# A two-layer encoder trunk on one core: the gates' way through HBM, all transposes of x in the norm's stretch, and two row blocks ordered by token half

## The chip, the cores and the metric

The kernel runs on one core of one Trainium2 chip. The metric is the device time of one execution in microseconds; the time shown is the median of several runs. TensorE (PE) multiplies; its weight loads are listed as PEld. VectorE (DVE) and ScalarE (ACT) do the element-wise work, SyncE (SP) and GpSimd (POOL) issue DMA transfers.

## The reference

256 tokens, model width 2048, two layers, all in float32. A conditioning vector gives six vectors per layer (shift, scale and gate for attention and for the MLP). Cut to what matters here:

```
cond = silu(c)
for l in range(2):
    sh_a, sc_a, g_a, sh_m, sc_m, g_m = split(cond @ w_ada[l] + b_ada[l], 6)
    h = rmsnorm(x) * (1 + sc_a) + sh_a
    proj = h @ w_in[l]                      # q, k, v of 4 differential heads; latents of 8 MLA heads
    out_a = diff_attention(...)             # two softmax maps per head, relative bias
    out_b = mla_attention(...)              # latent q and kv, rope
    x = x + g_a * (concat(out_a, out_b) @ w_o[l])
    h = rmsnorm(x) * (1 + sc_m) + sh_m
    x = x + g_m * (square(relu(h @ w_mlp_in[l])) @ w_mlp_out[l])
return rmsnorm(x) * final_norm_g
```

## The kernel before

**Precision.** Most products run as three matmuls on a faster 4-byte format: a weight block is split into a rounded high part (`hi`, made by ACT, line 151) and the rest (`lo`, made by DVE, line 154), and so is the activation; then hi·hi, hi·lo and lo·hi are added up. A weight block is 1 MB in a `raw` buffer (five of them, shared with the ada rows), and its parts live in four `hi` and four `lo` buffers of half a block each.

**Modulation.** The six vectors per layer come from `w_ada`: 192 rows of 1 MB, each loaded by SP (line 357), multiplied by the conditioning vector and summed on DVE (line 373), then added to the bias into `mod` (lines 385 and 387), 128 features per column. Loads are rationed: each call of `weights` adds a rate (`RATE_*`, by stage) to a credit in `more_ada`, and each whole credit loads one row; the sums are made at the next call.

**Row products.** The attention output projection (`w_o`) and the MLP's second product (`w_m2`) are made by `rows`: for each of four column groups `c` of 512, four weight blocks `kq`, and for both token halves `t` of 128 tokens (one PSUM bank each), eight high and four low matmuls of 512 columns per block and half (lines 309, 310, 312). Then `updates` multiplies by the gate row and adds to x on DVE (lines 1107, 1109), and ahead of a norm ACT squares the new x and sums it (line 1123). For the last column group (`last`), `first_squares` and `quiet` (no ada) apply, and in the last block all matmuls of half 0 come ahead of those of half 1. In this layout x has tokens on the partitions; `self.row` holds the gate on all 128 partitions, in the buffer that otherwise holds the relative bias.

**Gates.** `gate` brings `mod` (128 x 16) into HBM, element by element in transposed order, and reads it back over all partitions. Both transfers are POOL's. There are four of them: g_a and g_m of two layers.

**The norm between.** `norm_then_by_k` runs three times: ahead of the first MLP, of the second layer's attention and of the second MLP. x is turned back to features on partitions by PE transposes (line 1156; `turned(p)` makes four, for features 256 p to 256 p + 255, into one PSUM bank, and copies the bank to SBUF by ACT or DVE, lines 1165 and 1163). The root of each token half (`roots`: ACT square root, line 1137, DVE reciprocal, line 1140) is spread over the partitions by a matmul (`spread_one`, line 1144). `modulated` then makes h for 256 features: DVE scales (line 695), ACT adds the shift and rounds (line 698), DVE makes the rest (line 701). Eight such steps follow, each with its weight blocks: in layer 0 two blocks, by `by_k`; in layer 1 one, by `wide_by_k`, in which the low weights of all six banks come first in the very first step. Transposes 0 to 3 stand ahead of the second spread, 4 and 5 behind it and ahead of the first step's products, 6 and 7 one each ahead of the products of steps 1 and 2. PSUM has eight banks in rotation.

**Order.** The framework lists the instructions of each engine by its own cost model and the program's order, with transfers of SP among them: what is ready early can be issued ahead of its place in the program. `behind(a, b)` pins `a` behind `b` on an engine's list without a wait. Each engine then works its list in order.

**Start.** In the first layer x is loaded and turned ahead of the projection; for the residual it is loaded a second time with tokens on the partitions (line 976), and the relative bias is kept in HBM for layer 1 (line 974), by POOL.

**End.** `final` follows the last `rows`: last norm and eight output transfers of 128 x 512 values, four per token half.

Of the kernel before, what the change touches and what calls it, by code (L numbers as in the profile page):

```python
# [9 lines left out]
F32 = mybir.dt.float32  # L10
# [87 lines left out]
RATE_A0, RATE_V, RATE_A1, RATE_A2, RATE_K, RATE_K1, RATE_M = 1.1, 1.6, 0.5, 0.7, 0.6, 0.0, 0.66  # L98
# [3 lines left out]
class Trunk:  # L102
# [26 lines left out]
    def s(self, name, n=2):  # L129
        return self.sp.tile([P, n], F32, tag=f"s{n}", name=self.name(name))  # L130
# [60 lines left out]
    def mac(self, ps, w, c, m, x, first, last, shared=False):  # L191
        mm = self.nc.tensor.matmul
        hi, lo = w[0][:, c : c + m], w[1][:, c : c + m]
        mm(ps, hi, x[0], start=first, stop=False, skip_group_check=shared)  # L194
        mm(ps, hi, x[1], start=False, stop=False, skip_group_check=shared)  # L195
        self.last_mac = mm(ps, lo, x[0], start=False, stop=last, skip_group_check=shared)  # L196
# [48 lines left out]
    def by_k(self, banks, blocks, xs, k0, nk, n=4, whole=None):  # L245


        for b, (w, half) in enumerate(blocks):
            for i in range(len(w) * half // (n * P)):
                k = k0 + i  # L250
                for j in range(n):
# [7 lines left out]
                    else:  # L259
                        self.mac(ps, w[c // half], c % half, P, xs[k], first, last, True)  # L260
                if i == 0 and not whole:
                    self.last_mm = self.last_mac

    def wide_by_k(self, banks, blocks, xs, k0, nk):

        mm = self.nc.tensor.matmul
        n = len(banks)
        (w, half), = blocks
        for i in range(2 * half // (n * P)):
            k = k0 + i  # L270
            x, _, both = xs[k]
            part = lambda j, h: w[(i * n + j) * P // half][h][:, (i * n + j) * P % half :][:, :P]
            for h in (1, 0) if k == 0 else (0, 1):
                for j, ps in enumerate(banks):
                    if h:
                        mm(ps[:, 0], part(j, 1), x, start=k == 0, stop=k == nk - 1, skip_group_check=True)
                    else:
                        ins = mm(  # L278
                            ps.rearrange("p a b -> p (a b)"), part(j, 0), both, start=False, stop=False,
                            skip_group_check=True,  # L280
                        )
            if i == 0:
                self.last_mm = ins
# [12 lines left out]
    def rows_by_k(self, pss, src, xs, kq, apart=False):  # L296

        mm = self.nc.tensor.matmul
        w = self.weights(src)
        part = lambda i, h: w[i // 2][h][:, i % 2 * 512 : i % 2 * 512 + 512]  # L300
        for ts in ((0,), (1,)) if apart else ((0, 1),):
            for h in range(2):
                for i in range(4):
                    for t in ts:
                        ps = pss[t].rearrange("p a b -> p (a b)")
                        c = slice(t * P, (t + 1) * P)
                        xh, xl, _ = xs[4 * kq + i]
                        if h == 0:
                            mm(ps, xh[:, c], part(i, 0), start=kq == 0 and i == 0, stop=False)  # L309
                            mm(ps, xl[:, c], part(i, 0), start=False, stop=False)  # L310
                        else:
                            self.last_mm = mm(ps, xh[:, c], part(i, 1), start=False, stop=kq == 3 and i == 3)  # L312
# [375 lines left out]
    def modulated(self, x, r, k, sh, sc, after=None):  # L688
# [4 lines left out]
        for i, (hi, lo, _) in enumerate(out):  # L693
# [166 lines left out]
    def layer(self, l, acc=None):  # L860
# [112 lines left out]
        if l == 0:  # L973
            nc.gpsimd.dma_start(self.bias_kept, self.row)
            for t in range(2):
                nc.gpsimd.dma_start(self.xr[:, t], io["x"][t])
# [23 lines left out]
        self.rows_by_k(pss, io["w_o"][l, 0, 0], self.mo, 0)  # L1000
        for f in (av[0][1], av[1][1], av[2][0], av[3][0]):
            f()
        self.rows_by_k(pss, io["w_o"][l, 0, 1], self.mo, 1)
# [409 lines left out]
```

## Time and profile before

| | |
|---|---|
| median of 3 runs | 2195.16 us (2195.14 to 2196.54) |
| the profiled execution | 2194.0 us, its span 2191.8 us |
| PE busy | 2148.8 us, 98% of the span |
| DVE, ACT busy | 1590.6 us, 73%; 1141.8 us, 52% |
| HBM read, written | 589.66 MB, 3.18 MB |
| mean granted TensorE clock | 0.995 |

Matmuls run back to back nearly everywhere. The span holds, in order: the first norm and projection (to about 140 us), the rest of attention 0 with its output projection (to 413.5), norm and first MLP (to 1126.7), norm and attention 1 (to 1471.2), norm and second MLP (to 2182.4), last norm and output. A row of a group reads: line, engine, operation, output<-input, count, busy time; a bracket behind an instruction of the timeline holds the idle time of its engine before it and what ended it.

### The profile page before, as it was taken

How to read it: one execution, taken by the hardware profiler on the slowest of the kernel's cores; microseconds unless marked ns; L12 is line 12 of the kernel's file. 1: busy time of each engine (PE TensorE's matmuls, PEld its weight loads, DVE VectorE, ACT ScalarE, POOL GpSimd, SP SyncE). 2: the span in 40 equal slices, each digit the busy share in tenths (PEclk: the TensorE clock that was granted, in tenths of full speed). 3: DMA queues.
4: the chain of work that ended last, by engine and by line, in shares of the span. 5: the costliest groups of instructions: out<-in, count | busy, mean ns of one | idle time of the engine just before them, and what ended most of it. 6: DMA issues, size and time to landing. Idle time of an engine off the chain costs nothing.

```text
span 2191.8 us, 29356 instructions
## 1 busy us (share of the span) xinstructions
PE 2148.8 (98%) x11498; PEld 1861.3 (85%) x11498; DVE 1590.6 (73%) x2114; ACT 1141.8 (52%) x1724; POOL 11.1 (1%) x22
## 2 busy tenths in 40 slices
PE   7999999999999999999999999999999999999998
PEld 6899778898888888888889998888888888888886
DVE  7789778888778978887976776778655555555555
ACT  6555554555455355445454565547535534644643
POOL 0000000000000000000000000000000000000000
PEclk9999999999999999999999999999999999999999
DMA  9997898799988888889967766767864555555552
GB/s 386 423 386 290 258 354 323 287 342 344 289 329 333 326 304 322 328 305 295 346 231 259 260 234 228 261 222 251 296 235 175 202 196 179 192 200 184 192 196 93
DMA packets 87307, 594.76 MB, mean 271 GB/s; under 512 B 9984, under 2 KB 10368, under 8 KB 20352
## 3 DMA queue, kind: packets, MB, share of 16 engines
q1 hardware_dynamic: 85536, 583.93, 73.7%
q0 software_dynamic: 1344, 8.42, 1.0%
q8 instruction: 90, 1.47, 0.3%
q10 hardware_dynamic: 288, 0.52, 0.1%
q14 instruction: 49, 0.40, 0.0%
HBM read 589.66 MB, written 3.18 MB: 270 GB/s over the span
## 4 chain that ended last, share of the span: by engine, by line
PE 89%; DMA 5%; DVE 4%; ACT 1%; issue 1%; SPq 0%; ACTq 0%; DVEq 0%
PE ps L215 18%; PE pr L309 13%; PE pr L310 13%; PE pr L312 13%; PE ps L218 9%; PE pk L258 2%; PE pk L278 2%; PE pk L194 2%; PE pk L195 2%; PE pk L196 2%; DMA raw<-in_w_m 2%; DVE ada L373 1%; PE pv L293 1%; PE pv L294 1%; PE pv L292 1%; DMA w<-in_w_d 1%
## 5 line engine op out<-in xcount | busy, mean ns | idle before, releaser
L154 DVE TENSOR_TENSOR lo<-raw,hi 128x1024 fp32r<-128x1024 f32 (+1 forms) x714 | 836.0, 1195 | 434.4 <-issue 218.9
L151 ACT ACTIVATE hi<-raw 128x1024 fp32r<-128x1024 f32 (+1 forms) x714 | 733.4, 1036 | 724.2 <-PE pr L310 376.0
L373 DVE SCALAR_TENSOR_TENSOR ada<-ada,cond 128x2048 f32<-128x2048 f32 x192 | 438.7, 2287 | 17.9 <-DMA ada<-in_w_ada 17.5
L215 PE MATMUL ps<-h,hi 128*128 128x512 f32 x1856 | 432.1, 390 | 0.8 <-ACT hi L151 0.8
L215 PEld LDWEIGHTS ps<-h,hi 128*128 128x128 f32 x1856 | 344.9, 188 | 71.1 <-ACT hi L151 1.7
L310 PE MATMUL pr<-hi,hid 128*128 128x512 f32 x1024 | 398.5, 389 | 0.0
L309 PE MATMUL pr<-hi,hid 128*128 128x512 f32 x1024 | 398.4, 389 | 0.0
L312 PE MATMUL pr<-lo,hid 128*128 128x512 f32 x1024 | 253.2, 389 | 0.0
L218 PEld LDWEIGHTS ps<-h,lo 128*128 128x128 f32 x1856 | 230.3, 192 | 4.5
L218 PE MATMUL ps<-h,lo 128*128 128x256 f32 x1856 | 231.7, 283 | 0.0
L312 PEld LDWEIGHTS pr<-lo,hid 128*128 128x128 f32 x1024 | 192.2, 188 | 39.9
L310 PEld LDWEIGHTS pr<-hi,hid 128*128 128x128 f32 x1024 | 192.2, 188 | 39.7
L309 PEld LDWEIGHTS pr<-hi,hid 128*128 128x128 f32 x1024 | 192.2, 188 | 39.7
L194 PE MATMUL pk<-h,hi 128*128 128x256 f32 x320 | 90.3, 285 | 0.2 <-ACT h L698 0.2
L195 PE MATMUL pk<-h,hi 128*128 128x256 f32 x320 | 90.3, 283 | 0.0
L196 PE MATMUL pk<-h,lo 128*128 128x256 f32 x320 | 90.3, 283 | 0.0
L188 DVE TENSOR_TENSOR hid<-relu,hid 128x256 fp32r<-128x256 f32 x128 | 48.3, 422 | 57.0 <-ACT hid L187 57.0
L258 PE MATMUL pk<-hf,w 128*128 128x256 f32 x384 | 84.2, 380 | 3.6 <-DMA w<-in_w_d 3.6
L1175 ACT ACTIVATE sum<-ps 128x256 f32<-128x256 f32 x110 | 40.9, 379 | 89.1 <-PE ps L218 89.0
L258 PEld LDWEIGHTS pk<-hf,w 128*128 128x128 f32 x384 | 72.5, 190 | 14.2 <-issue 2.6
L1107 DVE TENSOR_TENSOR yg<-pr,bias 128x512 f32<-128x512 f32 x64 | 42.5, 685 | 30.0 <-PE pr L312 29.0
L194 PEld LDWEIGHTS pk<-h,hi 128*128 128x128 f32 x320 | 61.0, 192 | 0.6 <-ACT h L698 0.5
(236 smaller groups left out, 2495.5 us busy)
## 6 DMA issues: line engine op xcount, KB each, us to landing
raw<-in_w_m SPq DMA_DIRECT2D x238, 1024.0 KB, 5.6
ada<-in_w_ada SPq DMA_DIRECT2D x192, 1024.0 KB, 6.4
raw<-in_w_o SPq DMA_DIRECT2D x32, 1024.0 KB, 5.7
raw<-in_w_m SPq DMA_DIRECT2D x24, 768.0 KB, 5.7
raw<-in_w_dv SPq DMA_DIRECT2D x16, 1024.0 KB, 5.8
raw<-in_w_t SPq DMA_DIRECT2D x12, 1024.0 KB, 5.1
w<-in_w_a SPq DMA_DIRECT2D x24, 384.0 KB, 13.6
raw<-in_w_a SPq DMA_DIRECT2D x12, 768.0 KB, 4.9
```

The lines of the kernel that those rows point to most:

```text
L151: ins = self.nc.scalar.activation(hi, v, AF.Copy)
L154: ins = self.nc.vector.tensor_tensor(lo, v, hi.bitcast(F32), ALU.subtract)
L194: mm(ps, hi, x[0], start=first, stop=False, skip_group_check=shared)
L195: mm(ps, hi, x[1], start=False, stop=False, skip_group_check=shared)
L196: self.last_mac = mm(ps, lo, x[0], start=False, stop=last, skip_group_check=shared)
L215: mm(ps.rearrange("p a b -> p (a b)"), part(w, k, 0), x[2], start=k == 0, stop=False)
L218: mm(ps[:, 0], part(w, k, 1), x[0], start=False, stop=k == nk - 1)
L258: self.nc.tensor.matmul(ps, v, whole[k], start=first, stop=last, skip_group_check=True)
L309: mm(ps, xh[:, c], part(i, 0), start=kq == 0 and i == 0, stop=False)
L310: mm(ps, xl[:, c], part(i, 0), start=False, stop=False)
L312: self.last_mm = mm(ps, xh[:, c], part(i, 1), start=False, stop=kq == 3 and i == 3)
L373: ins = nc.vector.scalar_tensor_tensor(w, w, 1.0, self.cond, ALU.mult, ALU.mult, accum_out=acc[:, i : i + 1])
```

## The change

- `gate`: PE transposes `mod` into a PSUM bank, ACT copies the bank to SBUF, and POOL writes that to HBM as 16 rows of 512 bytes. The broadcast back is as before.
- `turned` is parted into `turn_in` (transposes) and `turn_out` (copy). In `norm_then_by_k` all eight sets of transposes stand ahead of the first step: 0, the first spread, 1 to 5, the second spread, 6, 7. ACT copies 5, 6 and 7 after the first step's h. DVE copies 1 and 3, ACT the others. Both parts of the first weight block are split without being held behind the last update of x (before: one, held). The call of `more_ada` in the first step goes.
- `by_k` in the first step (layer 0) starts the second block's tiles behind the last product of the first; `wide_by_k` (layer 1) does the first step in two groups of three banks.
- `rows`, for the last column group: blocks 2 and 3 are both split first; then half 0 with blocks 2 and 3, then half 1 with blocks 2 and 3.
- The bias kept and the second load of x are issued by SP in place of POOL.
- `RATE_M` is 0.7 in place of 0.66.

```diff
-RATE_A0, RATE_V, RATE_A1, RATE_A2, RATE_K, RATE_K1, RATE_M = 1.1, 1.6, 0.5, 0.7, 0.6, 0.0, 0.66
+RATE_A0, RATE_V, RATE_A1, RATE_A2, RATE_K, RATE_K1, RATE_M = 1.1, 1.6, 0.5, 0.7, 0.6, 0.0, 0.7
...
-    def mac(self, ps, w, c, m, x, first, last, shared=False):
+    def mac(self, ps, w, c, m, x, first, last, shared=False, after=None):
         mm = self.nc.tensor.matmul
         hi, lo = w[0][:, c : c + m], w[1][:, c : c + m]
-        mm(ps, hi, x[0], start=first, stop=False, skip_group_check=shared)
+        ins = mm(ps, hi, x[0], start=first, stop=False, skip_group_check=shared)
+        if after is not None:
+            self.behind(ins, after)
         mm(ps, hi, x[1], start=False, stop=False, skip_group_check=shared)
         self.last_mac = mm(ps, lo, x[0], start=False, stop=last, skip_group_check=shared)
...
-    def by_k(self, banks, blocks, xs, k0, nk, n=4, whole=None):
+    def by_k(self, banks, blocks, xs, k0, nk, n=4, whole=None, apart=False):
...
-                        self.mac(ps, w[c // half], c % half, P, xs[k], first, last, True)
-                if i == 0 and not whole:
-                    self.last_mm = self.last_mac
+                        other = self.last_mac if apart and b and i == 0 else None
+                        self.mac(ps, w[c // half], c % half, P, xs[k], first, last, True, other)
...
+        groups = [range(n)] if k0 else [range(n // 2), range(n // 2, n)]
+        last = None
+        for g in groups:
+            for i in range(2 * half // (n * P)):
+                k = k0 + i
+                x, _, both = xs[k]
+                part = lambda j, h: w[(i * n + j) * P // half][h][:, (i * n + j) * P % half :][:, :P]
+                for h in (1, 0) if k == 0 else (0, 1):
+                    for j in g:
+                        ps = banks[j]
+                        if h:
+                            ins = mm(ps[:, 0], part(j, 1), x, start=k == 0, stop=k == nk - 1, skip_group_check=True)
+                        else:
+                            ps = ps.rearrange("p a b -> p (a b)")
+                            ins = mm(ps, part(j, 0), both, start=False, stop=False, skip_group_check=True)
+                        if last is not None:
+                            self.behind(ins, last)
+            last = ins
...
-    def rows_by_k(self, pss, src, xs, kq, apart=False):
+    def rows_by_k(self, pss, w, xs, kq, ts=(0, 1)):
 
         mm = self.nc.tensor.matmul
-        w = self.weights(src)
...
     def rows(self, src, xs, c, last=False):
 
         pss = [self.bank("pr") for _ in range(2)]
-        for kq in range(4):
-            self.quiet = last and kq >= 2
+        for kq in range(2 if last else 4):
             if last and kq == 1:
                 self.first_squares()
-            self.rows_by_k(pss, src[c, kq], xs, kq, last and kq == 3)
+            self.rows_by_k(pss, self.weights(src[c, kq]), xs, kq)
+        if last:
+            self.quiet = True
+            w = [self.weights(src[c, kq]) for kq in (2, 3)]
+            for t in range(2):
+                for kq in (2, 3):
+                    self.rows_by_k(pss, w[kq - 2], xs, kq, (t,))
         return pss
...
+            if act is not None:
+                self.behind(self.last_h, act)
...
-        end, last_x = self.last_mm, self.last_x
+        end = self.last_mm
         raws = [self.raw(src[0, b], 1536) for b in range(2 - l)]
-        head, ins = self.part(raws[0], 0, 768, last_x)
+        parts = [self.part(raws[0], i, 768)[0] for i in range(2)]
         r, rb = self.s("rms"), self.bank("pn")[:, 0]
         x = [self.turned(0, end)]
         self.behind(self.last_square, self.last_turn)
-        root = []
-        for t in range(2):
-            root.append(self.roots(r, t))
-        self.behind(root[1][1], ins)
-        x.append(self.turned(1, self.last_turned, True, root[1][1]))
+        root = [self.roots(r, t) for t in range(2)]
+        self.spread_one(rb, r, 0, self.last_turned)
+        x.append(self.turned(1, self.last_spread, True, self.last_x))
+        self.behind(root[1][1], self.last_turn)
         x.append(self.turned(2, self.last_turned, False, root[1][0]))
-        self.spread_one(rb, r, 0, self.last_turned)
-        x.append(self.turned(3, self.last_spread, False, self.last_turn))
+        act = self.last_turn
+        x.append(self.turned(3, self.last_turned, True, root[1][1]))
+        x.append(self.turned(4, self.last_turned, False, act))
+        act = self.last_turn
+        late = [self.turn_in(i, self.last_turned) for i in (5,)]
         self.spread_one(rb, r, 1, self.last_turned)
-        spread = self.last_spread
+        late += [self.turn_in(i, self.last_spread) for i in (6, 7)]
         h, gate, banks = [], None, None
         for p in range(8):
             k = 2 * p
             for g in (sh, sc):
                 self.ada_need(l, g, k + 1)
-            new, ins = self.modulated(x[p], rb, k, self.mod[l, sh], self.mod[l, sc], gate)
+            new, ins = self.modulated(x[p], rb, k, self.mod[l, sh], self.mod[l, sc], gate, act if p == 0 else None)
             gate = None
             h += new
             if p == 0:
-                x += [self.turned(i, spread, False, self.last_h) for i in range(4, 6)]
+                x += [self.turn_out(ps, False, self.last_h) for ps in late]
                 banks = self.open_banks(6)
                 gate = ins, self.last_turn
-                parts = [head]
-                for i in range(1, 2 * len(raws)):
+                for i in range(2, 2 * len(raws)):
                     w, ins = self.part(raws[i // 2], i % 2, 768, ins)
                     parts.append(w)
-                self.more_ada(ins)
                 blocks = [(parts[2 * b : 2 * b + 2], 768) for b in range(len(raws))]
             else:
                 order = (self.last_h, ins) if p == 1 else None
                 blocks = self.by_k_weights([src[p, b] for b in range(2 - l)], 6, False, order)
-            if p in (1, 2):
-                x.append(self.turned(5 + p, self.last_mm, False, self.last_h))
             if l == 0:
-                self.by_k(banks, blocks, h, k, NK, 6)
+                self.by_k(banks, blocks, h, k, NK, 6, apart=p == 0)
             else:
                 self.wide_by_k(banks, blocks, h, k, NK)
         return h, banks
...
         if l == 0:
-            nc.gpsimd.dma_start(self.bias_kept, self.row)
+            nc.sync.dma_start(self.bias_kept, self.row)
             for t in range(2):
-                nc.gpsimd.dma_start(self.xr[:, t], io["x"][t])
+                nc.sync.dma_start(self.xr[:, t], io["x"][t])
...
-        self.nc.gpsimd.dma_start(d.rearrange("k p -> p k"), self.mod[l, g])
+        ps, m = self.bank("pg")[:NK, 0, :P], self.s("modT", P)
+        self.nc.tensor.transpose(ps, self.mod[l, g], self.ident)
+        self.nc.scalar.activation(m[:NK], ps, AF.Copy)
+        self.nc.gpsimd.dma_start(d, m[:NK])
...
-    def turned(self, p, after, by_dve=False, behind=None):
+    def turn_in(self, p, after):
...
+        return ps
+
+    def turn_out(self, ps, by_dve, behind):
+
...
+    def turned(self, p, after, by_dve=False, behind=None):
+        return self.turn_out(self.turn_in(p, after), by_dve, behind)
```

More of the change, by code (lines that the diff above doesn't have):

```diff
@@ L129, in s @@
     def s(self, name, n=2):
-        return self.sp.tile([P, n], F32, tag=f"s{n}", name=self.name(name))
+        return self.sp.tile([P, n], F32, tag=f"s{n}", name=self.name(name), bufs=8 if n < P else 1)
     def bank(self, name):
@@ L268, in wide_by_k @@
         (w, half), = blocks
[L269 to L283, printed above, removed]
+        groups = [range(n)] if k0 else [range(n // 2), range(n // 2, n)]
[16 more added lines that the diff above has]
+            last = ins
     def tokens_by_k(self, pss, w, xs, first, last):
@@ L294, in tokens_by_k @@
                 mm(ps, xl, hi, start=False, stop=last and k == len(xs) - 1)
-    def rows_by_k(self, pss, src, xs, kq, apart=False):
+    def rows_by_k(self, pss, w, xs, kq, ts=(0, 1)):
         mm = self.nc.tensor.matmul
-        w = self.weights(src)
         part = lambda i, h: w[i // 2][h][:, i % 2 * 512 : i % 2 * 512 + 512]
[L301 to L312, printed above, removed]
+        for h in range(2):
+            for i in range(4):
+                for t in ts:
+                    ps = pss[t].rearrange("p a b -> p (a b)")
+                    c = slice(t * P, (t + 1) * P)
+                    xh, xl, _ = xs[4 * kq + i]
+                    if h == 0:
+                        mm(ps, xh[:, c], part(i, 0), start=kq == 0 and i == 0, stop=False)
+                        mm(ps, xl[:, c], part(i, 0), start=False, stop=False)
+                    else:
+                        self.last_mm = mm(ps, xh[:, c], part(i, 1), start=False, stop=kq == 3 and i == 3)
     def rows(self, src, xs, c, last=False):
         pss = [self.bank("pr") for _ in range(2)]
-        for kq in range(4):
-            self.quiet = last and kq >= 2
+        for kq in range(2 if last else 4):
             if last and kq == 1:
                 self.first_squares()
-            self.rows_by_k(pss, src[c, kq], xs, kq, last and kq == 3)
+            self.rows_by_k(pss, self.weights(src[c, kq]), xs, kq)
[5 more added lines that the diff above has]
+                    self.rows_by_k(pss, w[kq - 2], xs, kq, (t,))
         return pss
@@ L686, in scaled, with modulated @@
         return out, lows, ins
-    def modulated(self, x, r, k, sh, sc, after=None):
+    def modulated(self, x, r, k, sh, sc, after=None, act=None):
         nc = self.nc
@@ L999, in layer @@
         pss = [self.bank("pr") for _ in range(2)]
[L1000 removed]
+        self.rows_by_k(pss, self.weights(io["w_o"][l, 0, 0]), self.mo, 0)
         for f in (av[0][1], av[1][1], av[2][0], av[3][0]):
             f()
[L1003 removed]
+        self.rows_by_k(pss, self.weights(io["w_o"][l, 0, 1]), self.mo, 1)
         av[2][1]()
@@ L1007, in layer @@
         for kq in (2, 3):
-            self.rows_by_k(pss, io["w_o"][l, 0, kq], o, kq)
+            self.rows_by_k(pss, self.weights(io["w_o"][l, 0, kq]), o, kq)
         self.updates(pss, 0, True)
```

## The prediction

> **What bounds the kernel now.** I read the page first (span and busy table), then the chain in order of time and the list of waits to find where PE stands still, then the busy time by windows around those places, then the timeline of each engine there. Rows of the page:
>
> ```profile
> span 2191.8 us, 29356 instructions
> PE 2148.8 (98%) x11498; PEld 1861.3 (85%) x11498; DVE 1590.6 (73%) x2114; ACT 1141.8 (52%) x1724; POOL 11.1 (1%) x22
> ```
>
> PE is the bound: it is idle 43 us of 2191.8, and only those, and PE work that could lie in them, can be won. The largest hole (windows; columns are PE, PEld, DVE, ACT, POOL busy, granted clock, DMA share, GB/s):
>
> ```profile
> 265.00:270.00 5.00, 5.00 (x24) 4.21 (x23) 4.29 (x6) 0.37 (x2) 0.00 (x0) 1.00 0.76 79
> 270.00:275.00 5.00, 1.33 (x6) 0.76 (x5) 0.00 (x0) 0.78 (x1) 0.54 (x1) 0.89 0.75 241
> 275.00:280.00 5.00, 3.07 (x7) 2.49 (x8) 4.51 (x5) 2.52 (x6) 0.00 (x0) 0.50 1.01 426
> 280.00:285.00 5.00, 5.00 (x24) 4.07 (x23) 1.07 (x6) 2.60 (x6) 0.00 (x0) 0.93 1.01 421
> 285.00:315.00 30.00, 30.00 (x141) 24.98 (x140) 25.68 (x35) 15.72 (x30) 0.00 (x0) 1.00 0.87 324
> ```
>
> PE idles 3.67 + 1.93 = 5.6 us, and then works at half clock for most of 3.07 us (1.5 us lost) and at 0.93 for 5 (0.35); with 0.15 at 0.89 that is 7.6 us. Why: the DMA engines are 0.76 busy and move 79 GB/s. The chain, page and POOL's rows name the cause:
>
> ```profile
> 259.55 14.59 DMA raw<-in_w_dv
> raw<-in_w_dv SPq DMA_DIRECT2D x16, 1024.0 KB, 5.8
> 257.61 1.18 POOL L1096 DMA_DIRECT2D gate<-mod  x1 [137.72 <-DVE mod L387]
> PE ps L215 <- ACT hi L151: 0.8, 2, 0.4
> ```
>
> A value-weight load issued 2 us behind the gate's write takes 14.59 us instead of 5.8; it is the chain's item there. The gate's write takes an 8 KB tile apart into 2048 elements of 4 bytes (`k p -> p k`). The other three gates meet more prefetch: PE waits on a weight block only 0.8 us, in two waits, and I put both down to late loads.
>
> **The change, part by part.** *Gates.* The scattered write becomes a PE transpose, an ACT copy and a contiguous write. Gone: 7.6 us at the first gate. Ends: half of it, 3.8, if the stage gives it back (DVE is 86% and DMA 0.87 busy in 285 to 315), or all. PE is 30.00 of 30.00 there, so neither is the bound, and I take -7.6. From the two small waits -0.8 (0 to -0.8). What comes new, and its cover:
>
> ```profile
> 414.83 0.39 PE L1144 MATMUL pn<-ident,rms 128*128 128x128 f32 x2
> 415.06 0.60 PE L1156 MATMUL tx<-ident,x 128*128 128x128 f32 x4
> L309 PEld LDWEIGHTS pr<-hi,mo x24: 187/188/190, 317.3 to 349.9; 128*128 128x128 f32 x24
> L1107 DVE TENSOR_TENSOR yg<-pr,bias x1: 682/682/682, 347.4 to 347.4; 128x512 f32<-128x512 f32 x1
> DMA to landing us min/median/max: 8.7/10.2/10.4
> ```
>
> The nearest PE operation is the spread (two records, 415.06 - 414.83 = 0.23 us): 4 x 0.23 = +0.9. The ACT copy lies beside matmuls: 0. The broadcast of the gate over the partitions (the landing row, 10.2) now starts near the output projection, at 317.3, and is used at 347.4; with the contiguous 8 KB write bounded by another 10.2, that needs 20.4 of those 30 us. Without that cover it would cost its landing time. PE's wait for the modulation is the slower rival below.
>
> *Turns.* All 32 transposes of x now lie between the last row matmul and the first projection matmul:
>
> ```profile
> 413.52 1.47 PE L1156 MATMUL tx<-ident,x 128*128 128x128 f32 x12
> 416.47 0.49 PE L1144 MATMUL pn<-ident,rms 128*128 128x128 f32 x2 [0.82 <-DVE rms L1140]
> 416.80 1.04 PE L1156 MATMUL tx<-ident,x 128*128 128x128 f32 x8
> 413.72 0.69 DVE yg L1107
> 415.18 0.73 ACT sq L1123 x2
> 416.42 0.59 DVE xT L1163
> 418.07 0.86 PE pk L194 x5
> 1135.54 0.60 PE L1156 MATMUL tx<-ident,x 128*128 128x128 f32 x4
> 1135.90 1.64 PE L278 MATMUL pk<-h,hi 128*128 128x512 f32 x6
> ```
>
> That stretch lasts 4.55 us (413.52 to 418.07) and is set by the chain gated sum, square, root, reciprocal, xT copy, modulation, which the change keeps in length: DVE copies turn 3 where it copied turn 1, at 416.42 to 417.01. Before, PE does 24 transposes and two spreads in it. New: 32 at (414.83 - 413.52)/12 = 0.109 is 3.5, plus 0.23 and 0.33 for the spreads, 4.05 us: it fits with 0.5 to spare, and the second spread (24 transposes and a spread from 413.52: 416.4) is not pushed past the 416.47 of its reciprocal. Saved: the two later turns, 1135.90 - 1135.54 = 0.36 each, in three norms: -2.2. Banks: eight hold pn, one row bank and six turns; the row bank is read by 414.41 (413.72 + 0.69) and turn 0 copied before ACT's square at 415.18, both before turns 6 and 7 want theirs at 416.8. Three late turns keep banks until ACT has copied them; the first weight half needs only three.
>
> *More ada taken out of the norm's first step.* Third norm:
>
> ```profile
> 1481.84 0.50 PE L278 MATMUL pk<-h,hi 128*128 128x512 f32 x1 [1.26 <-ACT hi L151]
> 1477.36 2.29 DVE L373 SCALAR_TENSOR_TENSOR ada<-ada,cond 128x2048 f32<-128x2048 f32 x1
> 1475.71 0.85 PE L276 MATMUL pk<-h,lo 128*128 128x256 f32 x5 [0.24 <-ACT h L698]
> ```
>
> The 2.29 us sum delays step 1's modulation, so ACT splits its weights late and PE waits 1.26. It moves one step on, where DVE is ahead by the weight split that now lies before the norm: I take -0.9 (0 to -1.3). Raising the M rate from 0.66 to 0.7 moves loads earlier: 0.
>
> *Halves of banks.* In layer 1 the first step issues three low matmuls instead of five or six before it needs the low half of h; two of 0.85/5 = 0.17 us of cover are gone, 0.34 at most: 0.25 in each of two norms, +0.5 (0 to +0.7).
>
> *Token halves.* The last two blocks run token half 0 first, so both must be split earlier:
>
> ```profile
> 402.19 4.63 DVE L154 TENSOR_TENSOR lo<-raw,hi 128x1024 fp32r<-128x1024 f32 x4
> 402.41 0.19 PEld L309 LDWEIGHTS pr<-hi,do 128*128 128x128 f32 x1
> 410.05 0.91 PE pr L312 x4
> ```
>
> A row matmul takes 0.91/4 = 0.227. Block 2 starts at 402.6; block 3's first low is now wanted 20 matmuls later, 407.2, and is made by 402.19 + 3 x 1.16 = 405.7; the second is wanted at 407.6 and made by 406.8. It fits by 0.8: 0, with +1.5 as the other end should one 1.2 us split slip past it. Token 0 ends 12 x 0.227 = 2.7 us earlier and its update leaves DVE and ACT free; token 1's chain is as long as before.
>
> *Tail.* That also brings two of the eight 256 KB outputs out 2.7 us sooner:
>
> ```profile
> 2184.00:2190.00 6.00, 0.00 (x0) 0.00 (x0) 2.24 (x5) 2.26 (x5) 0.00 (x0) 0.62 0.95 351
> ```
>
> DMA is 0.95 busy to the end, so 512 KB at 351 GB/s is 1.5 us less in the queue, but token 1's own issue follows: -0.8 (0 to -1.5).
>
> *Bias and x on SP.* Three 1 MB transfers leave POOL's queue for SP's. The first norm is where DMA is full:
>
> ```profile
> 95.00:100.00 5.00, 2.73 (x13) 2.14 (x12) 3.20 (x6) 1.71 (x4) 0.00 (x0) 1.00 1.01 414
> 88.51 0.54 POOL L974 DMA_DIRECT2D bias_kept<-bias  x1 [21.67 <-ACT bias L565]
> PE pk L258 <- DMA w<-in_w_d: 3.6, 2, 2.3
> 80.32 17.18 DMA w<-in_w_d
> L1054 SPq DMA_DIRECT2D cond<-in_fg x1: 662/662/662, 1577.2 to 1577.2; - x1
> ```
>
> The bias write, issued at 88.51, runs beside weights issued from 80.32 that PE then waits 2.3 us for, the longer of two waits of 3.6 us. In one queue it would stand behind them: 1 MB at 414 GB/s is 2.5 us. The scheduler hoists SP transfers into gaps (the `fg` row: at 1577.2, though its place in the program is behind the last MLP block's first output columns), so I don't expect the x loads to leave this stretch. Ends: -3.6 (both waits go) and +3 (SP stands for a release and weights behind it come late). I take half the first wait, -1.2.
>
> The Trainium skill speaks against this term: *DMA: Bandwidth & Descriptors*, section "Issuing engines are not separate DMA queues", says that transfers of all issuing engines run on the same 16 DMA engines and interleave, so that another issuer saves issue time only. By it the move is worth 0 and the sum is -10.9, which gives 2184.
>
> **Sum.** -7.6 - 0.8 + 0.9 - 2.2 - 0.9 + 0.5 + 0 - 0.8 - 1.2 = -12.1. The profiled execution took 2194.0 us (span 2191.8 and 2.2 around it): 2181.9. The median of the three runs, 2195.16, is 1.2 above it: 2183.
>
> **The rivals.** *The first gate's hole is given back* (17%). For: DVE 86% and DMA 0.87 busy behind it. Against: PE without a gap there. Half back: -8.3, 2187. *The turns lengthen the norm* (12%): the first spread needs token 0's root, and if its reciprocal sits on DVE behind token 1's update (done by 415.18, when the square begins), PE stands some 1.2 us from turn 0's end near 414.0 with the turns behind it, in three norms: +3.6, 2187. Against: with token 0 done 2.7 us earlier its root is ready long before.
>
> *Slower: PE waits where POOL waited* (6%).
>
> ```profile
> POOL gate L1096 <- DVE mod L387: 1123.4, 4, 389.0
> ada<-in_w_ada SPq DMA_DIRECT2D x192, 1024.0 KB, 6.4
> ```
>
> POOL's wait for the modulation cost nothing; a transpose at PE's queue head holds every matmul behind it. If it is placed when the last ada load is just issued, it waits 6.4 + 2.29 = 8.7 us; two gates so placed cost 17 and turn the sum to +5, 2200.5; from 12 us in all it decides. Against: the sums for the first gate end at 257.6, 60 us before the output projection. *That the write is not the cause* of the late load: its two terms are gone and -3.7 stays, 2191.5 (5%).
>
> **How the numbers follow.** The forecast, sum within its ends, 60%, own range 2178 to 2187. With the rivals at 2187 the range reaches 2177 to 2190: it leaves out the slower case, the case without cause, and a little on the low side, 2 in 10. A measurement of this kernel can tell about 0.2%, 4.4 us, from no change: faster is below 2190.8. Faster 0.86 (forecast, both rivals at 2187, part of the unnamed rest); same 0.08; slower 0.06.
>
> **What would show it.** Right: no PE hole near 270 and no clock of 0.50 there; no DMA stretch at 79 GB/s; 32 transposes between the last row matmul and the first projection matmul, which still start 4.3 to 4.6 us after it; none later; no 1.26 us wait in the third norm; first outputs 2.7 us ahead. Wrong: PE waiting at the gate's transpose, late splits in the last two blocks, or longer waits for `w_d` and `w_a` in the first 140 us.

## The result, and the profile after

The changed kernel takes 2178.82 us (median of four runs, 2177.42 to 2180.82) against 2195.85 us for the kernel before on the same chip (2195.14 to 2197.27): ratio 0.9922 [0.9905, 0.9939], 17.0 us less. On a second chip it took 2178.46 against 2194.15: 0.9929 [0.9915, 0.9942], 15.7 us less. The forecast was 2183, range 2177 to 2190: right in sign and in range, with a time 4.2 us above the measured one. One execution of e2, below, took 4371 us, twice the others, and the ratio given for e2 leaves it out.

The profiled execution took 2180.82 us, the slowest of its four. The page after (span, then busy time):

```profile
span 2178.8 us, 29359 instructions
PE 2147.1 (99%) x11502; PEld 1860.6 (85%) x11502; DVE 1592.7 (73%) x2117; ACT 1143.1 (52%) x1725; POOL 6.8 (0%) x19
```

PE's idle time fell from 43.0 us to 31.7. The second of the two waits for `w_d` before the change, as a window (columns: PE, PEld, DVE, ACT, POOL busy, granted clock, DMA share, GB/s):

```profile
130.00:135.00 5.00, 3.69 (x20) 3.15 (x19) 4.69 (x11) 1.71 (x4) 0.00 (x0) 1.00 1.03 430
```

The windows after, where the gate's hole and the two waits for `w_d` stood:

```profile
95.00:100.00 5.00, 5.00 (x25) 4.41 (x24) 0.26 (x1) 0.73 (x3) 0.00 (x0) 1.00 1.04 429
130.00:135.00 5.00, 5.00 (x28) 4.37 (x27) 4.86 (x11) 4.48 (x6) 0.00 (x0) 1.00 1.01 423
265.00:270.00 5.00, 5.00 (x24) 4.19 (x24) 4.90 (x10) 1.78 (x4) 0.00 (x0) 1.00 0.97 372
270.00:275.00 5.00, 5.00 (x26) 4.27 (x25) 2.41 (x5) 3.31 (x9) 0.00 (x0) 1.00 0.97 352
275.00:280.00 5.00, 5.00 (x24) 3.96 (x23) 4.91 (x10) 4.14 (x10) 0.00 (x0) 1.00 0.57 223
```

No PE hole near 270, no clock of 0.50, no stretch at 79 GB/s; and both waits of the first norm are gone (PE 2.73 of 5 at 95 and 3.69 at 130 before, 5.00 at both now). The first matmuls after the first norm between, in the timeline:

```profile
405.28 1.08 PE L314 MATMUL pr<-lo,do 128*128 128x512 f32 x4
406.19 0.60 PE L1166 MATMUL tx<-ident,x 128*128 128x128 f32 x4
406.63 0.39 PE L1154 MATMUL pn<-ident,rms 128*128 128x128 f32 x2
406.85 2.35 PE L1166 MATMUL tx<-ident,x 128*128 128x128 f32 x20
409.15 0.49 PE L1154 MATMUL pn<-ident,rms 128*128 128x128 f32 x2
409.47 1.04 PE L1166 MATMUL tx<-ident,x 128*128 128x128 f32 x8
410.75 0.50 PE L194 MATMUL pk<-h,hi 128*128 128x256 f32 x2 [0.24 <-ACT h L705]
```

All 32 transposes (4 + 20 + 8) and both spreads lie ahead of the first projection matmul, which starts 4.56 us after the turns begin (410.75 - 406.19); before it was 4.55. The 0.82 us wait for the second root's reciprocal is filled with transposes.

**The lead.** To see where time goes I pair each matmul with the matmul of the same name and number in the trace of before and subtract their starts. At the turns of the first norm between, for example, 413.52 - 406.19 = 7.33 us. Each row is a place, by its time in before; a step from one row to the next is what that stretch won or lost. The last row is the difference of the spans.

| us in before, place | changed | changed, second chip (e5) | gate only (e1) | gate as rows (e6) | norm only (e3) | SP only (e9) |
|---|---|---|---|---|---|---|
| 42, first projection | 1.1 | 0.6 | 0.4 | 0.6 | 0.8 | 0.8 |
| 132, end of it | 5.3 | 4.8 | 0.7 | 0.6 | 0.6 | 5.0 |
| 246, value projection | 3.6 | 2.9 | 0.8 | 0.7 | 0.8 | 1.8 |
| 312, behind the hole | 11.6 | 10.8 | 8.5 | 8.3 | 0.2 | 2.7 |
| 413.3, output projection done | 7.3 | 10.5 | 8.4 | 7.8 | 0.2 | 2.4 |
| 455, past norm 1 | 8.0 | 11.2 | 8.4 | 7.8 | 0.9 | 2.5 |
| 1125, MLP done | 9.3 | 12.5 | 9.7 | 9.3 | 0.1 | 3.5 |
| 1378, past norm 2 | 10.0 | 13.2 | 9.6 | 9.3 | 0.9 | 3.5 |
| 1471, attention 1 done | 10.0 | 13.2 | 9.5 | 9.3 | 1.0 | 3.5 |
| 1661, past norm 3 | 12.2 | 15.3 | 9.4 | 9.3 | 3.2 | 3.5 |
| span | 13.0 | 16.1 | 10.0 | 9.3 | 3.2 | 4.3 |

The changed kernel's first profile loses 4.3 us between 312 and 413, in short waits for weights in the output projection; the second execution of the same kernel (e5) loses 0.3 there, and two kernels that are the same up to this place or nearly so lose 1.7 (e7) and 0.8 (e8). So the loss differs from execution to execution, and e5 is the one to sum by.

### The profile page after: what moved, and what is told of

Read it like the earlier page. It is cut to its first block, busy times and chain, and to the rows that moved or that the text cites. A ratio compares the mean times of both kernels' runs of the same rounds, so it can differ in the third digit from the quotient of the medians.

```text
span 2178.8 us, 29359 instructions
## 1 busy us (share of the span) xinstructions
PE 2147.1 (99%) x11502; PEld 1860.6 (85%) x11502; DVE 1592.7 (73%) x2117; ACT 1143.1 (52%) x1725; POOL 6.8 (0%) x19
## 4 chain that ended last, share of the span: by engine, by line
PE 94%; DVE 2%; DMA 2%; ACT 1%; issue 0%; SPq 0%; ACTq 0%
PE ps L217 19%; PE pr L314 13%; PE pr L311 13%; PE pr L312 13%; PE ps L220 10%; PE pk L260 3%; PE pk L284 2%; PE pk L194 2%; PE pk L198 2%; PE pk L197 2%; PE pv L296 1%; PE pv L297 1%; PE pv L298 1%; DMA raw<-in_w_o 1%; PE pk L281 1%; PE ps L197 1%
## 5 line engine op out<-in xcount | busy, mean ns | idle before, releaser
L198 PEld LDWEIGHTS pk<-h,lo 128*128 128x128 f32 x320 | 61.4, 192 | 0.2 <-DVE lo L154 0.2
```

## The experiments

The kernel before took 2193.2 us on the chip of e1 to e4, 2194.15 on that of e5 to e8, and 2193.19 on that of e9 to e12.

### The parts alone: e1, e2, e3

e1 is the kernel before with the new `gate`. e2 is the kernel before with this edit alone:

```diff
-            nc.gpsimd.dma_start(self.bias_kept, self.row)
+            nc.sync.dma_start(self.bias_kept, self.row)
             for t in range(2):
-                nc.gpsimd.dma_start(self.xr[:, t], io["x"][t])
+                nc.sync.dma_start(self.xr[:, t], io["x"][t])
```

e3 is the changed kernel with the old `gate` and with POOL's transfers.

> The kernel before with the new gate alone (PE transpose, ACT copy, contiguous write). Theory A, the scattered write starves the weight loads: the hole near 270 us goes (5.6 us of idle PE and 2 us at a lower clock), the stage behind it keeps the lead, the two small waits of the MLP (0.6 each) go too; time 7 to 9 us under the kernel before. Rival B, the lead is handed back in the output projection of layer 0, because the loads there are short in any case: the lead after the hole is 7.7 us but only about 4 at 413 us, time 3.5 to 5 us under before.

> The kernel before with the bias kept and the second load of x issued by SP alone. Theory A: both transfers leave the first norm's stretch (they go out at 164 and 185 us), the two waits for w_d of 2.5 and 1.5 us at 97 and 132 us go, so that the kernel leads by 4 to 5 us at 140 us; the x load then delays the up-projections' weights near 185 to 215 us and 2 to 4 us of that are lost again; time 0 to 3 us under before. Rival B, moving transfers between issuing queues changes nothing (all share the same DMA engines): the lead is below 1 us at 140 us and the time within 1 us of before.

> The changed kernel with the old gate and the old POOL transfers: turns, halves, first-step groups, ada moved and the M rate are left. Theory A: 0.7 us per norm, 1.5 more in the third, 0.8 at the tail: time 4 to 5 us under before. Rival B, the halves cost what the turns bring: a wait of 0.6 us or more for the split of the last block in layer 0's output projection, time 2 to 3 us under before.

Measured: e1 2184.2 us, 0.9955 [0.9943, 0.9966], 9.0 us less; e2 2190.54, 0.9982 [0.9973, 0.9990], 2.7 less; e3 2191.09, 0.9991 [0.9982, 0.9999], 2.1 less. They add up to 13.8 of 15.7 to 17.0, and e3 falls short of the 4 to 5 expected. In the table e1 goes from 0.8 to 8.5 at the hole and keeps 8.4 to 413: nothing is given back, which was the first rival. It wins 1.3 more in the MLP up to 1125. That part is not shown to be the gates': e9, which still scatters every gate, wins 1.0 there. e3 shows the norms by themselves: 0.7, 0.8 and 2.2. It gives 1.5 us back ahead of 995, where PE waits 2.00 us for a split weight, behind a gate's write at 973.78 that it still scatters; the load it waited for took 15.83 us. So what a scattered write costs in the MLP depends on whether PE is about to need the load that it holds up: 2.00 us in e3, two waits of 0.4 in the kernel before, none in e9. For e2 the times alone are used, and e9 was made for the trace.

### Is it the scatter? e6, the gate in 128 contiguous rows

```diff
-        d = self.dp.tile([NK, P], F32, name=f"gate{l}{g}")
-        self.nc.gpsimd.dma_start(d.rearrange("k p -> p k"), self.mod[l, g])
-        flat = d.rearrange("k p -> (k p)").unsqueeze(0)
+        d = self.dp.tile([P, NK], F32, name=f"gate{l}{g}")
+        self.nc.gpsimd.dma_start(d, self.mod[l, g])
+        flat = d.rearrange("p k -> (p k)").unsqueeze(0)
```

> The kernel before with the gate written to HBM as 128 contiguous rows of 64 bytes, in place of 2048 scattered elements; no PE transpose, no ACT copy. The gate's values come out in another order, so the result is not the reference's. Theory A, the number of 4-byte pieces is the whole cause of the hole: no hole near 270 us, DMA over 200 GB/s from 260 to 275 us, time 8 to 10 us under before, as with the new gate alone, and 0 to 1 us below that since PE is spared four transposes. Rival B, any small write from POOL in front of the weight loads (its wait for HBM, or its place in the value stage) makes the hole: half or more of it stays, time at most 4 us under before.

In this kernel the gate's values reach x in another order, so its output is not the reference's; the transfers and the work are the same in size. Measured: 2185.1 us, 0.9961 [0.9948, 0.9973], 9.0 us less, as e1. POOL's timeline, the windows and the DMA issues of e6:

```profile
256.87 0.55 POOL L1096 DMA_DIRECT2D gate<-mod  x1 [137.58 <-DVE mod L387]
```

```profile
265.00:270.00 5.00, 5.00 (x24) 4.21 (x23) 4.99 (x8) 3.03 (x4) 0.00 (x0) 1.00 0.97 401
270.00:275.00 5.00, 5.00 (x24) 4.14 (x23) 4.03 (x9) 1.54 (x5) 0.00 (x0) 1.00 1.00 416
```

```profile
gate<-mod POOLq DMA_DIRECT2D x4, 8.0 KB, 5.8
```

The same row before:

```profile
gate<-mod POOLq DMA_DIRECT2D x4, 8.0 KB, 15.8
```

The write goes out at the same place (256.87; before 257.61), beside the same loads, with the same 8 KB, and no PE transpose. Written as rows the DMA engines move 401 and 416 GB/s where they moved 79 and 241, and PE has no hole. That singles out the scatter: neither the moment of the write nor its engine is the cause. Whether it is the size of the pieces or their distance in HBM (4 bytes, 512 apart, against rows of 64) is not told apart. The Trainium skill, *DMA: Bandwidth & Descriptors*, section "Rules for kernel authors", says that a non-contiguous last dimension lowers to one descriptor per element and advises a contiguous one; the gain here agrees with the advice. The trace's count of packets under 512 B hardly changes (9984 before, 9856 here), so that count does not show the elements.

### The same again, the third norm, and x later: e5, e7, e8

e5 is the changed kernel. e7 puts `self.more_ada(ins)` back into the norm's first step. e8 issues the second load of x (SP, as in the change) in the middle of the value projection, ahead of its fifth block.

> The changed kernel once more, timed on the same chip as the next three and profiled a second time. Theory A: the 2.3 us of lead that its first profile lost in layer 0's output projection (waits of 0.6 to 1.2 us for weight loads at 313, 318, 377, 389 and 395 us) were that execution's own, as its time was the highest of four: the second profile loses less than 1 us there, and the time lies 14 to 17 us under before. Rival B: the loss belongs to the kernel (the gate's 1 MB broadcast at 316 us stands in the way of the weights): the same waits stand there again.

> The changed kernel with the call of more_ada back in the first step of the three norms. Theory A, the 2.29 us sum in that step is what makes PE wait in the third norm: a wait of about 1.3 us returns some 10 us after that norm's transposes begin, nothing in the other two norms, time 1 to 2 us over the changed kernel. Rival B, the wait went because all turns are ahead of the first step (ACT no longer has turns 6 and 7 between h and the weight splits): no wait returns, time within 0.5 us of the changed kernel.

> The changed kernel with the second load of x moved on, from ahead of the q up-projection (issued at 185 us) to the middle of the value projection. Theory A, at 185 us its 2 MB delay the up-projection weights and cost the waits of 2.1 and 1.0 us between 205 and 216 us: lead over before at 229 us rises from 3.8 to 5 or more us, and the value stage, whose DMA share is 0.84, takes the 2 MB without a wait: time 1 to 3 us under the changed kernel. Rival B, the value stage is as full: PE waits there instead, time within 1 us of the changed kernel or above it.

Measured: e5 2178.46 us (above); e7 2180.09, 0.9938 [0.9925, 0.9950]; e8 2175.31, 0.9914 [0.9900, 0.9927], 3.1 us less than e5 and the fastest yet. For e7 the timeline of PE and the group of the sum on DVE in the third norm:

```profile
1462.16 0.60 PE L1167 MATMUL tx<-ident,x 128*128 128x128 f32 x4
...
1471.98 1.65 PE L284 MATMUL pk<-h,hi 128*128 128x512 f32 x6 [0.65 <-ACT hi L151]
```

```profile
L380 DVE SCALAR_TENSOR_TENSOR ada<-ada,cond x1: 2282/2282/2282, 1467.5 to 1467.5; 128x2048 f32<-128x2048 f32 x1
```

With the call back, the sum runs at 1467.5, 5.3 us behind the turns' start (1462.16), and PE waits 0.65 us. In the changed kernel it runs 9.7 us behind it, and PE goes through the same stretch without a wait but the first 0.24 (timelines of PE, then of DVE):

```profile
1461.12 0.60 PE L1166 MATMUL tx<-ident,x 128*128 128x128 f32 x4
...
1465.67 0.62 PE L281 MATMUL pk<-h,lo 128*128 128x256 f32 x3 [0.24 <-ACT h L705]
1466.19 1.66 PE L284 MATMUL pk<-h,hi 128*128 128x512 f32 x6
1467.68 0.87 PE L281 MATMUL pk<-h,lo 128*128 128x256 f32 x6
1468.39 1.54 PE L284 MATMUL pk<-h,hi 128*128 128x512 f32 x6
```

```profile
1470.77 2.29 DVE L380 SCALAR_TENSOR_TENSOR ada<-ada,cond 128x2048 f32<-128x2048 f32 x1
```

e7's lead grows by 0.9 from 1471 to 1661, the changed kernel's by 2.1: the call is worth 1.2 of the 2.1. Nothing was expected in the other two norms, but norm 2 has the same wait 9.8 us behind its turns' start (1117.71):

```profile
1127.47 1.66 PE L284 MATMUL pk<-h,hi 128*128 128x512 f32 x6 [0.56 <-ACT hi L151]
```

e7's lead stays at 9.0 over norm 2 (1125 to 1378), where the changed kernel wins 0.7. So there the early turns win nothing as long as the call stays; in norm 1 e7 wins the 0.7.

For e8 the reading starts in the changed kernel. Groups of the two lines on SP, and two rows of its list of waits:

```profile
L981 SPq DMA_DIRECT2D bias_kept<-bias x1: 425/425/425, 164.2 to 164.2; - x1
L983 SPq DMA_DIRECT2D x<-in_x x2: 436/520/604, 185.2 to 185.7; - x2
```

```profile
PE pss L194 <- ACT hi L151: 2.1, 1, 2.1
PE pss L198 <- DVE lo L154: 1.0, 2, 0.5
```

The 3 MB did leave the first norm: SP issues them at 164 and 185, in attention. There PE then waits 3.1 us for split weights, and the lead falls from 5.3 to 3.6. In e8 SP issues x at 219 and 244 and both waits are absent:

```profile
L1003 SPq DMA_DIRECT2D x<-in_x x2: 423/427/431, 219.2 to 244.1; - x2
```

Its lead is 4.9 at 132 and 5.6 at 246, and 13.2 behind the hole against 10.8 in e5.

### Queue or time? e9 and e10

e9 is e2's kernel again. e10 is e6's (with the gates' values in another order, too) with POOL still issuing the three transfers, but behind the first gate's write:

```diff
-        self.nc.gpsimd.dma_start(d, self.mod[l, g])
+        ins = self.nc.gpsimd.dma_start(d, self.mod[l, g])
+        if l == 0 and g == 2:
+            self.behind(self.nc.gpsimd.dma_start(self.bias_kept, self.row), ins)
+            for t in range(2):
+                self.behind(self.nc.gpsimd.dma_start(self.xr[:, t], self.io["x"][t]), ins)
```

> The kernel before with the bias kept and the second load of x issued by SP, once more, for its profile. Theory (the gain is the time at which the 3 MB run): the two waits for w_d, 3.6 us, are gone, the lead over before is 3.5 to 4.5 us at the start of head products (near 174), 1.5 to 2 of it is lost at 200 to 230 behind the x loads that SP issues near 185, and 2 to 3 are kept to the end: 2191 to 2192. Rival (SP's order of weights, not the time of the transfers): the w_d waits stay and the lead comes elsewhere, behind 140. By the rule of the skill's page DMA: Bandwidth & Descriptors, that another issuer saves issue time only, the lead is 0 throughout.

> The kernel before with the gate written as 128 rows of 64 bytes (its values come in another order) and with POOL still issuing bias and x, but behind the first gate's write, near 257. If the gain of the move is the time at which the 3 MB run, POOL does as well as SP: the waits for w_d go and the lead is about 4 us at 132; behind 257 the three 1 MB transfers share the engines with weights at 0.9 to 1.0 busy and may cost 0 to 2.5 us (1 MB at 414 GB/s each, less what prefetch covers): 2180 to 2184 against 2185.1 of the gate rows alone. If it is SP's queue that matters, the lead at 132 stays under 1 us and the time is 2185 or above.

Measured: e9 2189.57 us in one run (3.6 below the before of that chip); e10 2189.54, 0.9981 [0.9972, 0.9990], 3.7 us less than before but some 5 behind e6 and outside the 2180 to 2184 expected. The windows of e9, then of e10, around the first norm's two waits:

```profile
95.00:100.00 5.00, 5.00 (x25) 4.41 (x24) 0.00 (x0) 0.00 (x0) 0.00 (x0) 1.00 1.03 420
130.00:135.00 5.00, 5.00 (x26) 4.32 (x26) 4.83 (x11) 4.80 (x7) 0.00 (x0) 1.00 1.02 429
```

```profile
95.00:100.00 5.00, 5.00 (x25) 4.38 (x25) 0.00 (x0) 0.00 (x0) 0.00 (x0) 1.00 1.03 427
130.00:135.00 5.00, 5.00 (x30) 4.45 (x29) 4.86 (x10) 3.88 (x5) 0.00 (x0) 1.00 1.02 429
```

Both waits are gone in both, and the lead between 42 and 132 grows by 4.2 us in e9 (0.8 to 5.0) and by 4.1 in e10 (1.8 to 5.9). SP as an issuer has no part in it: what counts is that 3 MB no longer share a stretch that already runs at 414 to 431 GB/s. The Trainium skill's section weighed in the prediction is borne out in its mechanism (the issuer brings no bandwidth) and not in the conclusion drawn from it there, a worth of 0: changing the issuer also changed the time of issue, and e2's ratio of 0.9982 [0.9973, 0.9990] is what that was worth. By e9's leads only 1.0 us of it is left at 246 (0.8 at 42, 5.0 at 132, 1.8 at 246); the rest of its 4.3 comes behind that, in places where nothing was moved, and which of it belongs to the move is not shown.

e10 then pays at the other end. POOL's timeline, the windows, and the one item of the chain:

```profile
252.95 0.69 POOL L1092 DMA_DIRECT2D gate<-mod  x1 [170.16 <-DVE mod L387]
253.63 0.53 POOL L1094 DMA_DIRECT2D bias_kept<-bias  x1
254.16 1.08 POOL L1096 DMA_DIRECT2D x<-in_x  x2
```

```profile
260.00:265.00 5.00, 5.00 (x24) 4.16 (x23) 4.65 (x8) 0.60 (x2) 0.00 (x0) 1.00 1.03 434
265.00:270.00 5.00, 3.98 (x18) 3.06 (x17) 3.72 (x5) 3.30 (x6) 0.54 (x1) 1.00 1.01 423
275.00:280.00 5.00, 2.70 (x12) 1.88 (x10) 0.00 (x0) 0.34 (x1) 0.00 (x0) 0.97 1.02 429
280.00:285.00 5.00, 2.29 (x5) 1.85 (x6) 3.55 (x7) 2.88 (x6) 0.00 (x0) 0.50 0.61 226
285.00:290.00 5.00, 5.00 (x22) 4.16 (x21) 4.78 (x8) 2.91 (x6) 0.00 (x0) 0.85 0.81 270
```

```profile
264.60 15.04 DMA raw<-in_w_dv
```

A hole as in before, at nearly the same place: a value load takes 15.04 us, PE idles 6.0 us in these windows and runs at 0.50 behind it, and the lead over before, which has its own hole here, falls from 4.7 to 4.0 between 246 and 312, where e6's rises from 0.7 to 8.3. So the hole costs some 8 us; I had priced it at 0 to 2.5. The signature is another one, though: 423 to 434 GB/s at a share of 1.0, where the scattered write left 79 GB/s at 0.76. The one is too many bytes at once, the other a transfer in small pieces.

### The token halves: e11 and e12

e11 is e8 again; e12 is e8 with the last two row blocks as before the change (blocks 0 to 2 for both halves, and half 0 first in block 3 alone).

> The changed kernel with the second load of x in the middle of the value projection, again, beside the next one. 2175 to 2176; ratio 0.991 to 0.992.

> The same with the last two row blocks as before (half 0 first in the last block only). Prediction's view (token halves free, output 2.7 us ahead): 0.8 us slower than the one beside it, up to 1.5, in the last 6 us. Rival (the outputs' end hangs on token half 1, which the order does not move): the same within 0.5 us, and the stretch from the last product to the end as long in both. If the earlier splits cost in the output projections: up to 1.5 us faster, with a shorter way from 380 to 413.

Measured: e11 2175.8 us (2174.02 to 2176.15), 0.9916 [0.9903, 0.9930]; e12 2175.65 (2174.79 to 2176.93), 0.9918 [0.9904, 0.9931]: no difference in the times. e4 had asked the same of the changed kernel itself:

> The changed kernel with the last two row blocks as before: block 2 with both token halves, then block 3 half by half. Theory A, the halves only free DVE and ACT ahead of the norm and bring the first outputs out sooner: the tail gains back 0.8 us less, the wait of 0.57 us at 395 us in layer 0's output projection goes, norms as in the changed kernel or up to 0.5 us longer each; time within 1.5 us of the changed kernel. Rival B, the norm's short stretch rests on token half 0 being done early (its root would otherwise be late for the first spread and hold the turns): each norm 1.2 us longer, time 3 to 5 us over the changed kernel.

Measured: 2179.63 us, 0.9934 [0.9922, 0.9946], beside e5's 0.9929 on another chip: inside the intervals. The output rows of e11, then of e12:

```profile
L1096 SPq DMA_DIRECT2D out_y<-x x2: 343/344/344, 2162.0 to 2162.6; - x2
L1096 ACTq DMA_DIRECT2D out_y<-x x2: 339/358/377, 2167.4 to 2168.0; - x2
```

```profile
L1093 SPq DMA_DIRECT2D out_y<-x x2: 343/344/344, 2165.2 to 2165.8; - x2
L1093 ACTq DMA_DIRECT2D out_y<-x x2: 338/357/376, 2167.9 to 2168.6; - x2
```

The last matmul of the rows starts at 2163.52 in e11 and 2164.04 in e12. The first output is issued 1.5 us before it in e11 and 1.2 us behind it in e12: 2.7 us sooner, as predicted. The last output is issued 4.5 us behind it in both. From that matmul to the end of the span it is 8.7 to 9.0 us in five profiles with the new order and 9.8 in e3, the sixth (mean 9.0), and 9.0 to 9.8 in the seven without it (mean 9.4). So the earlier outputs are worth some 0.4 us in the mean at most, and the times of e11 and e12 do not show it.

The traces show a second effect, in the first norm between alone. Without the order by halves PE stands ahead of the first spread (e12):

```profile
400.89 0.49 PE L1159 MATMUL pn<-ident,rms 128*128 128x128 f32 x2 [0.42 <-DVE rms L1155]
```

The first projection matmul then starts 5.02 us behind the turns in e12 and 5.03 in e4, against 4.55 to 4.56 in all norms of the kernels with the order, and norm 1 wins 0.2 in place of 0.7. Norms 2 and 3 keep their 4.55 to 4.56 without it. So e4's rival was right in its mechanism, in one norm of three and at 0.5 us in place of 1.2.

## Why the prediction was right, point by point

The sign, the range and the main mechanism were right. The steps, by e5's leads (16.1 us of span) against the prediction's 12.1:

| step | predicted | measured | by |
|---|---|---|---|
| gate's hole | -7.6 | -7.6 to -7.9 | e1, e6; e5 2.9 to 10.8 |
| two small MLP waits | -0.8 | -1.3, not shown to be the gates' | e1, e5, 455 to 1125; e9 -1.0 |
| four PE transposes | +0.9 | 0.1 each where seen | e1 against e6, 1125 to 1661 |
| later turns, three norms | -2.2 | -0.7 each in norms 1 and 2, not by the turns alone | e3, e5; e4, e12, e7 |
| ada out of the third norm's first step, less the halves of banks | -0.9 and +0.5 | -1.4 together | e5 2.1, less 0.7 for the turns |
| tail | -0.8 | -0.8, not shown to be the halves' | e5 (15.3 to 16.1), e12 |
| bias and x on SP | -1.2 | -2.7; by leads from 42 to 246 -2.3 and -1.0 | e2; e5, e9 |

**Right.** The gate's hole was the scattered write, wholly, and was not given back. The turns fitted into the norm as worked out: the first projection matmul starts 4.56 us behind the turns against a predicted 4.55, and each norm wins the 0.7 us of the two late turns. That took two of the other edits: the halves for 0.5 of it in norm 1, and the call of `more_ada` taken out for all of it in norm 2. The prediction names the first as its reason against the rival of the longer norm; it put the second in the third norm alone. PE never waited at a gate's transpose: POOL's write was at 309.86 in place of 257.61 and its broadcast, issued at 316.68 and 7.2 us on its way in the median, was there when the first gated sum began at 338.1.

**The mis-sized term: bias and x on SP.** The step that failed is the sentence that the scheduler would hoist the loads of x into gaps, so that they would not leave the first norm; from it I took half of one wait. They went to 185 and bias to 164, both `w_d` waits went (4.2 us from 42 to 132), and about 1.9 of them came back as `pss` waits behind the moved loads (e5, 132 to 246). That leaves -2.3 in e5; e2's times say -2.7 for the whole. In e9 4.2 went and 3.2 came back, so that the -1.0 left at 246 is near the -1.2 forecast: that is luck, as neither part of it was foreseen. The bounds I gave, -3.6 to +3, held all three; the mechanism within them was wrong. The `fg` row from which I argued is a load for a free buffer; what held x back in the list of SP was not settled by any run.

**Smaller terms.** The price of 0.23 us for a gate's transpose came from a spread of two matmuls; where e1 can be read against e6 it is 0.08 to 0.11 (the steps of e1's lead at 687, 1377 and 1568). The halves of banks cost nothing that can be seen: norm 2, which has them, gains 0.7 like norm 1, which has not; no run has them alone. For the third norm's sum I took 0.9 of a 1.26 us wait, and it all went; e7 puts 1.2 on the call. For the order by halves I took 0 outside the tail; it is 0.5 in norm 1. Most of the terms that missed erred to the same side, so that the measured time lies only 0.8 us above the low end of the forecast's own range (2178).

**The rivals.** Given back: refuted by e1 (8.5 at 312, 8.4 at 413). Turns lengthen the norm: not so in the changed kernel, by the timeline above; without the order by halves it happens in norm 1 (0.5 us, e4 and e12). PE waits where POOL waited, the slower one: no such wait in any profile. The write not the cause: refuted by e6 for the hole.

**Open.** The 4.3 us that the changed kernel's first profile lost in the output projection, and e5's did not: no run varies what could set it, and the four runs of that kernel span only 3.4 us. The 1.3 us in the MLP, of which e9 wins 1.0 without the new gate. Also the lead of 0.4 to 1.8 us at 42, which even kernels unchanged there have.

## What to carry to other kernels

Where a load takes two and a half times its usual time, read the GB/s beside the DMA share before choosing the cure. Here 79 GB/s at a share of 0.76 was a transfer in small pieces, cured by making it contiguous (e6 shows that contiguity alone does it; the transpose is what keeps the values in order), while 430 GB/s at 1.0 was too many bytes at once, cured by moving bytes to a stretch with room. It is the GB/s that tells them apart: behind the second gate's write, from 595 to 600 us in the kernel before, the share was 1.34 at 133 GB/s. Handing a transfer to another issuer is a change of its time; look where it lands, as the two loads of x were worth 3 us more at 219 and 244 than at 185. And undo each part alone, and read each place where it could act: the largest by lines here, the norm's reordering, was worth 2.1 us by itself (3.4 by e5's leads), and three changed lines of a DMA's access pattern were worth 9. Parts can also need each other, as the early turns need the halves in norm 1 and the removed call in norm 2.

## What the runs showed of the hardware

- An 8 KB write that the program asks for in 2048 elements of 4 bytes held up 1 MB loads beside it for some 10 us (79 and 241 GB/s in two windows, one load 14.59 us in place of 5.8); the same bytes in 128 rows of 64 bytes did not (401 and 416), and landed in 5.8 us instead of 15.8 (medians of four writes).
- The granted clock fell to 0.50 behind idle stretches of 5.6 us (before) and 5.0 us (e10, 2.30 + 2.71 in two windows that meet), while the 2.1 us wait of the changed kernel for `pss` at 214 left it at 1.00, in these windows:

```profile
210.00:215.00 5.00, 2.63 (x20) 2.21 (x18) 2.82 (x7) 4.06 (x7) 0.00 (x0) 1.00 0.76 313
215.00:220.00 5.00, 4.74 (x39) 4.74 (x40) 5.00 (x5) 1.32 (x2) 0.00 (x0) 1.00 0.52 172
```
